# Rows of A and R copied by DMA inside SBUF in place of ScalarE copies

## The chip, the cores and the metric

The kernel runs on one core of one Trainium2 chip. The metric is the device time of one execution, in microseconds (us). A core has five engines that run side by side, each with its own in-order instruction stream: TensorE (PE in the profile, its weight loads PEld), VectorE (DVE), ScalarE (ACT), GpSimd (POOL) and SyncE (SP), which here only issues DMA transfers. Sixteen DMA engines move data between HBM and the on-chip memory SBUF, and within SBUF. TensorE writes into PSUM.

## What is computed

A trunk of two residual layers on 256 positions of width 2048. The first layer is a bidirectional RWKV-7 mixer of width 4096 (64 heads of 64), the second a chunked gMLP, and a final RMSNorm closes. The change lies in the first layer, whose core is a recurrence on a 64x64 state per head and direction:

```python
def step(S, inp):
    r_t, w_t, k_t, v_t, a_t, b_t = inp
    sa = jnp.einsum('bhvk,bhk->bhv', S, a_t)
    S = (S * w_t[:, :, None, :]
         + sa[..., None] * b_t[:, :, None, :]
         + v_t[..., None] * k_t[:, :, None, :])
    y = jnp.einsum('bhvk,bhk->bhv', S, r_t)
    return S, y
```

Here r, k and v come from one input projection (with a mix of neighbouring positions), w and a-related rates from two low-rank projections, a is -kk, b is kk times a rate, and the two directions use their own w and rates. The outputs are normalised per head, a bonus term is added, the result is gated and projected back to 2048.

## The kernel before

The recurrence runs in chunks of 64 positions. Within a chunk it becomes matrix products: for a batch of four heads (two 128-row tiles, `l`), two directions (`d`) and four chunks (`c`) there are 16 units for each of the two heads that share a tile (`h`). There are 16 such batches, and each passes through three steps one period apart, so that in a period batch p gets its weights projected and its factors made (`mains`, `rates`, `factors`, `early_grams`), batch p-1 is made ready for the recurrence (`before`, `values`, `transposed_factors`) and batch p-2 runs it (`after`, which is `chain` and `finish`).

The names that matter:

- `AR` holds the scaled A rows (q = 0) and R rows (q = 1) of a batch. Head h lies in partitions 64h to 64h+63 (`H[h]`), and the last two axes are q and 64 positions, so one unit's A or R row is 64 floats, 256 bytes, on a partition. It has two buffers.
- `grams` multiplies `BK` with `AR` on TensorE (`gp`, line 584) and VectorE masks the product into `Gs` (line 589), which has 2C = 128 columns for each unit and two buffers.
- `inverses` (line 611 on) copies quarter blocks of `Gs` out with ScalarE (`Dt`, line 623, and `NQ`, line 624) and builds from them the inverse `TTs` of a unit-triangular matrix; VectorE does its substitution in 31 pairs of instructions (`TD` and `X`, lines 639 and 641). Once the blocks are out, the upper 64 partitions' first 64 columns of `Gs` are free and get the A rows (line 633).
- `values` (line 666 on) transposes V into the lower half of `SUV` and puts the R rows into `RC` (line 684), of which there is one.
- `chain` goes through the four chunks. In each it forms `xp` from `Gs` (A rows above, masked products below) and `SUV` (line 713), copies it to `Xs` with ScalarE (718), forms `uu` with `TTs` (722), copies that into `SUV` (724), forms the state `sp` (729) and the outputs `yp` (716 with `RC`, from the second chunk on, and 731), and carries the state on through `SJ` (736 to 741).

Weights come as f32 tiles `raw_w...` of 512 KB by SyncE's queue (line 145), are cut into a high and a low part by a ScalarE cast (`whi`, 150) and a VectorE subtraction (`wlo`, 151), and TensorE multiplies three products for each pair (lines 165 to 167). There are two raw buffers in this stage and three of each part, so a load is let go by the subtraction of the load two before it. Each batch has four projections (k, r, v, g) of four loads each, and one smaller load `wu`.

The code is written as generators that yield planned times, and a scheduler with a timeline model then sets the order of each engine's instructions. The order is fixed when the program is built; at run time an engine goes through its own list and waits at semaphores.

Of the kernel before, what the change touches and what calls it, by code (L numbers as in the profile page):

```python
# [22 lines left out]
def trunk(tc, x, norm_g, final_norm_g, w_in, mu_prev, mu_next, w0, w_up, a0, a_up, k_k, k_a, r_k,  # L23
          ln_w, ln_b, w_out, g_w_in, g_ln_g, g_ln_b, g_w_s, g_b_s, g_w_out, out):
    nc = tc.nc
    V, S, G, PE = nc.vector, nc.scalar, nc.gpsimd, nc.tensor
# [9 lines left out]
    C = 64  # L36
# [23 lines left out]
    def sm(name, tag="pg", bufs=2):  # L60
        return psm.tile([P, 512], F32, tag=tag, name=name, bufs=bufs)
# [250 lines left out]
    H = [slice(0, 64), slice(64, 128)]  # L312
# [31 lines left out]
    RC = c2.tile([P, 2, 16, C], F32, name="RC")  # L344
# [266 lines left out]
    def inverses(b, f):  # L611

        Gs, AR = f["Gs"], f["AR"]

        def lane(name):
            return se.tile([P, 16 * 33], F32, tag="ln", name=f"{name}{b}", bufs=3)

        Dt = lane("Dt")[:, :512].rearrange("p (t u) -> p t u", u=16)
        NQ = sc.tile([P, 16, 32], F32, tag="vy", name=f"NQ{b}", bufs=2)
        for h in range(2):  # L620
            for q in range(2):
                r0 = h * 64 + q * 32
                S.copy(Dt[r0:r0 + 32].rearrange("p t u -> p u t"), Gs[q * 32:q * 32 + 32, h, :, q * 32:q * 32 + 32])
            S.copy(NQ[h * 64:h * 64 + 32], Gs[0:32, h, :, 32:64])
        yield TSUB[0]
        La = se.tile([P, 32, 32], F32, tag="La", name=f"La{b}")
        V.transpose(La, Dt.unsqueeze(2).to_broadcast([P, 32, 2, 16]))
        xs = lane("X")
        G.memset(xs[:, :512], 0.0)
        G.tensor_scalar(xs.rearrange("p (m r) -> p m r", r=33)[:, :, 0:32:16], diag, 1.0, None, ALU.mult)  # L630
        X = xs[:, :512].rearrange("p (s t) -> p s t", t=16)
        for h in range(2):
            S.copy(Gs[H[0], h, :, 0:C], AR[H[h], :, :, :, 0].rearrange("p d l c t -> p (d l c) t"))
        TD = lane("TD")[:, :512]
        for j in range(31, 0, -1):
            yield TSUB[1] - (TSUB[1] - TSUB[0] - 2) * j / 31
            m, n = j // 2, 16 - j // 2
            tv = TD[:, :j * n].rearrange("p (s t) -> p s t", t=n)
            V.tensor_tensor(tv, La[:, j, 0:j].unsqueeze(2).to_broadcast([P, j, n]),  # L639
                            X[:, j:j + 1, m:].to_broadcast([P, j, n]), ALU.mult)  # L640
            V.tensor_tensor(X[:, 0:j, m:], X[:, 0:j, m:], tv, ALU.add)  # L641
        yield TSUB[1]
        Tn = lane("Tn")[:, :512]
        V.transpose(TD.rearrange("p (u t h) -> p t h u", t=16, h=2), X.rearrange("p s t -> p t s"))
        V.transpose(Tn, TD)
        TD, Tn = [t.rearrange("p (u t) -> p u t", t=32) for t in (TD, Tn)]
        qp = sm(f"qp{b}", "pq", 1).rearrange("p (u t) -> p u t", t=32)
        R0 = [slice(h * 64, h * 64 + 32) for h in range(2)]
        R1 = [slice(h * 64 + 32, h * 64 + 64) for h in range(2)]
        yield TQ[0]  # L650
        for u in range(16):
            for h in range(2):
                PE.matmul(qp[R1[h], u], NQ[R0[h], u], Tn[R0[h], u], start=True, stop=True)
        for h in range(2):
            S.copy(NQ[R1[h]], qp[R1[h]])
        yield TQ[1]
        for u in range(16):
            for h in range(2):
                PE.matmul(qp[R0[h], u], NQ[R1[h], u], TD[R1[h], u], start=True, stop=True)
        yield TQ[1] + 2  # L660
        for h in range(2):
            S.copy(TTs[R0[h], h, :, 32:64], qp[R0[h]])
            S.copy(TTs[R0[h], h, :, 0:32], TD[R0[h]])
            S.copy(TTs[R1[h], h, :, 32:64], TD[R1[h]])

    def values(b, f):

        yield 72
        Vt = f["Vt"]
        SUV = sc.tile([P, 2, 2, NC, 2, C], F32, tag="SUV", name=f"SUV{b}")  # L670
        G.memset(SUV[H[0], :, :, 0].rearrange("p d l h v -> p (d l) (h v)"), 0.0)
        vp = sm(f"vp{b}", "pq", 1).rearrange("p (m n) -> p m n", n=P)
        for cl in range(2):
            for tt in range(TT):
                PE.transpose(vp[:, cl * TT + tt], Vt[:, cl, tt * P:(tt + 1) * P], ident)
        for d in range(2):

            rows_ = SUV[H[1], d].rearrange("p l c h n -> p (l c) (h n)")
            if d == 1:
                rows_ = rows_[:, ::-1]  # L680
            for half in range(2):
                S.copy(rows_[:, half::2], vp[H[half]])
        for h in range(2):
            S.copy(RC[H[0], h], f["AR"][H[h], :, :, :, 1].rearrange("p d l c t -> p (d l c) t"))
        f.update(SUV=SUV)

    def chain(b, f):
# [99 lines left out]
    def before(b, f):  # L787
        yield from grams(b, f, 1)
        yield from inverses(b, f)
# [119 lines left out]
    for p in range(NB + 2):  # L909
        act = [mains(plan[p], st) if p <= NB else early_out()]  # L910
        if p == 0:
            act.append(low_rank())
        if p < NB:
            act += [rates(p, st[p]), factors(p, st[p]), early_grams(p, st[p])]
        if 0 < p <= NB:
            act += [before(p - 1, st[p - 1]), values(p - 1, st[p - 1]), transposed_factors(p - 1, st[p - 1])]
        if p > 1:
            act.append(after(p - 2, st[p - 2]))
        act = [[0.0, i, g] for i, g in enumerate(act)]
        while act:  # L920
            cur = min(act, key=lambda a: a[:2])
            try:
                cur[0] = max(cur[0], next(cur[2]))
            except StopIteration:
                act.remove(cur)
# [204 lines left out]
    for tt in range(TT):  # L1130
        rstd2 = rms(total(part2[:, tt:tt + 1], f"ssq2_{tt}", hp), f"rstd2_{tt}", hp, V)
        for m in range(NM):
            h = h1[m][:, tt]
# [37 lines left out]
```

## Time and profile before

| | us |
|---|---|
| median of three timed runs | 2244.96 |
| lowest and highest of them | 2243.38, 2249.34 |
| the profiled execution's own time | 2240.81 |
| its span, first to last instruction | 2238.7 |
| granted TensorE clock, mean | 0.993 |
| line 633, ScalarE copy Gs<-AR, each | 1.04 |
| line 684, ScalarE copy RC<-AR, each | 1.05 |
| line 150, cast of one weight tile, each | 1.05 |
| weight load of 512 KB, issue to landing | 3.7 to 3.8 |

The recurrence stage, with all copies of lines 633 and 684, runs from about 88 to 1305 us of the span. Behind it come the rest of the output projection and the second layer. A row of the timeline or of the chain of waits has the start in us, the length in us, the engine, the line and the operation or tile; a bracket at its end tells how long the engine was idle before it and what ended that. A group's row has the busy time in us and the mean length in ns, and behind the second bar the idle time before it. A row of the waits has the engine and line that waited, what ended the wait, the us in total, the times and the longest.

### The profile page before, as it was taken

To read this page: it belongs to the slowest core of one execution; us is meant where nothing else is said; L and a number is where in the kernel's file an instruction comes from. 1 tells how busy PE (TensorE), PEld (TensorE's weight loads), DVE (VectorE), ACT (ScalarE), POOL (GpSimd) and SP (SyncE) were. 2 spreads that over 40 slices of the span, in tenths; PEclk is the share of its full clock that TensorE was granted. 3 is DMA by queue.
4 is the path that set the end of the run, shared out by engine and by line. 5 is a ranking of instruction groups with operands and counts; after the bars stand their busy time and mean duration, and the time that the engine had idled before them with its cause. 6 is when DMAs were issued, how large, how long until landed. Compare 5 with 4: busy or idle time off the path is not lost.

```text
span 2238.7 us, 48543 instructions
## 1 busy us (share of the span) xinstructions
PE 2185.6 (98%) x19984; PEld 1949.8 (87%) x19984; DVE 1613.5 (72%) x3121; ACT 1403.4 (63%) x2192; POOL 188.9 (8%) x230
## 2 busy tenths in 40 slices
PE   7999999999999999999999999999999999999998
PEld 7898899989999999999999977778888888888886
DVE  5787688878877977887797774475546777777444
ACT  6657777777768777776877774464444444444443
POOL 2210100101011101101110100000000000000000
PEclk9999999999999999999999999999999999999999
DMA  5444234333334344434344455586776666666664
GB/s 165 137 129 130 82 113 119 98 108 116 115 115 119 112 125 117 121 109 127 110 121 117 140 175 183 177 262 190 215 213 191 195 193 197 189 193 197 194 196 156
DMA packets 286126, 339.22 MB, mean 152 GB/s; under 512 B 11600, under 2 KB 233552, under 8 KB 285776
## 3 DMA queue, kind: packets, MB, share of 16 engines
q1 hardware_dynamic: 265648, 314.88, 46.5%
q10 hardware_dynamic: 20256, 21.24, 3.3%
q8 instruction: 157, 2.57, 0.5%
q14 instruction: 65, 0.53, 0.1%
HBM read 329.78 MB, written 6.29 MB: 150 GB/s over the span
## 4 chain that ended last, share of the span: by engine, by line
PE 70%; ACT 10%; DMA 9%; DVE 8%; issue 3%; POOL 0%; ACTq 0%; SPq 0%; POOLq 0%; DVEq 0%
PE uacc L204 5%; PE gacc L204 5%; DMA raw_o<-in_rwkv_w_out_dram 4%; PE oacc L166 3%; PE oacc L167 3%; PE oacc L165 3%; PE gp L584 3%; PE uacc L206 3%; PE gacc L206 3%; PE vacc L166 3%; PE vacc L167 3%; PE vacc L165 3%; PE accv L166 3%; PE accv L167 3%; PE accv L165 2%
## 5 line engine op out<-in xcount | busy, mean ns | idle before, releaser
L204 PE MATMUL uacc<-z,whi_u 128*128 128x512 f32 x512 | 179.0, 394 | 0.0
L204 PE MATMUL gacc<-z,whi_g 128*128 128x512 f32 x512 | 177.3, 393 | 0.0
L165 PE MATMUL accv<-zh,whi_wv 128*128 128x256 f32 x512 | 151.8, 296 | 7.0 <-ACT whi_wv L150 7.0
L165 PE MATMUL acck<-zh,whi_wk 128*128 128x256 f32 x512 | 150.9, 295 | 1.4 <-ACT whi_wk L150 1.4
L167 PE MATMUL acck<-zh,wlo_wk 128*128 128x256 f32 x512 | 148.5, 290 | 3.1 <-DVE wlo_wk L151 3.1
L167 PE MATMUL accv<-zh,wlo_wv 128*128 128x256 f32 x512 | 150.5, 294 | 0.8 <-DVE wlo_wv L151 0.5
L166 PE MATMUL accv<-zl,whi_wv 128*128 128x256 f32 x512 | 150.9, 295 | 0.0
L165 PE MATMUL accg<-zh,whi_wg 128*128 128x256 f32 x512 | 150.2, 293 | 0.0
L167 PE MATMUL accg<-zh,wlo_wg 128*128 128x256 f32 x512 | 148.8, 291 | 0.5 <-DVE wlo_wg L151 0.5
L167 PE MATMUL accr<-zh,wlo_wr 128*128 128x256 f32 x512 | 148.4, 290 | 0.2 <-DVE wlo_wr L151 0.2
L166 PE MATMUL acck<-zl,whi_wk 128*128 128x256 f32 x512 | 147.4, 288 | 0.0
L165 PE MATMUL accr<-zh,whi_wr 128*128 128x256 f32 x512 | 146.8, 287 | 0.3 <-ACT whi_wr L150 0.3
L166 PE MATMUL accg<-zl,whi_wg 128*128 128x256 f32 x512 | 146.1, 285 | 0.0
L166 PE MATMUL accr<-zl,whi_wr 128*128 128x256 f32 x512 | 146.0, 285 | 0.0
L206 PE MATMUL uacc<-z,wlo_u 128*128 128x256 f32 x512 | 142.4, 284 | 0.0
L206 PE MATMUL gacc<-z,wlo_g 128*128 128x256 f32 x512 | 140.2, 279 | 0.0
L151 DVE TENSOR_TENSOR wlo_v<-raw_v,whi_v 128x1024 fp32r<-128x1024 f32 x64 | 78.4, 1225 | 80.4 <-ACT whi_v L150 80.4
L151 DVE TENSOR_TENSOR wlo_o<-raw_o,whi_o 128x1024 fp32r<-128x1024 f32 x64 | 78.2, 1224 | 77.7 <-ACT whi_o L150 77.5
L639 DVE TENSOR_TENSOR TD<-La,X 128x126 f32<-128x126 f32 (+22 forms) x496 | 125.6, 253 | 11.2
L641 DVE TENSOR_TENSOR X<-X,TD 128x126 f32<-128x126 f32 (+22 forms) x496 | 124.9, 252 | 10.0
L151 DVE TENSOR_TENSOR wlo_p<-raw_p,whi_p 128x1024 fp32r<-128x1024 f32 x60 | 73.9, 1231 | 75.7 <-ACT whi_p L150 75.7
L150 ACT CAST whi_p<-raw_p 128x1024 fp32r<-128x1024 f32 x60 | 63.1, 1051 | 91.5 <-PE oacc L167 87.3
(333 smaller groups left out, 6936.9 us busy)
## 6 DMA issues: line engine op xcount, KB each, us to landing
raw_wk<-in_rwkv_w_in_dram SPq DMA_DIRECT2D x64, 512.0 KB, 3.8
raw_wr<-in_rwkv_w_in_dram SPq DMA_DIRECT2D x64, 512.0 KB, 3.7
raw_wv<-in_rwkv_w_in_dram SPq DMA_DIRECT2D x64, 512.0 KB, 3.7
raw_wg<-in_rwkv_w_in_dram SPq DMA_DIRECT2D x64, 512.0 KB, 3.7
raw_o<-in_rwkv_w_out_dram SPq DMA_DIRECT2D x64, 512.0 KB, 3.8
raw_v<-in_gmlp_w_in_dram SPq DMA_DIRECT2D x64, 512.0 KB, 3.7
raw_u<-in_gmlp_w_in_dram SPq DMA_DIRECT2D x64, 512.0 KB, 3.5
raw_g<-in_gmlp_w_in_dram SPq DMA_DIRECT2D x64, 512.0 KB, 3.6
```

What stands on the lines that cost most here:

```text
L150: latest[0] = S.copy(hi, raw)
L151: latest[1] = V.tensor_tensor(lo, raw, hi.bitcast(F32), ALU.subtract)
L165: PE.matmul(acc, a[0], b[0], start=first, stop=False, skip_group_check=True)
L166: PE.matmul(acc, a[0], b[1], start=False, stop=False, skip_group_check=True)
L167: PE.matmul(acc, a[1], b[0], start=False, stop=last, skip_group_check=True)
L204: PE.matmul(acc.rearrange("p h t -> p (h t)"), hi[:, j, cs], zc[:, k].rearrange("p h t -> p (h t)"), start=k == 0, stop=False, skip_group_ ...
L206: PE.matmul(acc[:, 0], lo[:, j, cs], zc[:, k, 0], start=False, stop=k == KT - 1, skip_group_check=True)
L584: PE.matmul(gp[h][:, c].rearrange("p q t -> p (q t)"), BK[H[h], d, cl, c].rearrange("p q t -> p (q t)"), AR[H[h], d, cl, c].rearrange("p q ...
L639: V.tensor_tensor(tv, La[:, j, 0:j].unsqueeze(2).to_broadcast([P, j, n]), X[:, j:j + 1, m:].to_broadcast([P, j, n]), ALU.mult)
L641: V.tensor_tensor(X[:, 0:j, m:], X[:, 0:j, m:], tv, ALU.add)
```

## The change

The four ScalarE copies of a batch, two of A rows (line 633) and two of R rows (line 684), go. Four DMA transfers take their place, issued from SyncE's queue at the end of `values`, one for each head h and for A and R. Each moves 64 partitions of 16 rows of 256 bytes, 256 KB, from `AR` to `Gs` or `RC`, all inside SBUF.

```diff
         X = xs[:, :512].rearrange("p (s t) -> p s t", t=16)
-        for h in range(2):
-            S.copy(Gs[H[0], h, :, 0:C], AR[H[h], :, :, :, 0].rearrange("p d l c t -> p (d l c) t"))
         TD = lane("TD")[:, :512]
...
                 S.copy(rows_[:, half::2], vp[H[half]])
+
         for h in range(2):
-            S.copy(RC[H[0], h], f["AR"][H[h], :, :, :, 1].rearrange("p d l c t -> p (d l c) t"))
+            for dst, q in ((f["Gs"][H[0], h, :, 0:C], 0), (RC[H[0], h], 1)):
+                nc.sync.dma_start(dst, f["AR"][H[h], :, :, :, q].rearrange("p d l c t -> p (d l c) t"))
         f.update(SUV=SUV)
```

The scheduler orders the transfers like other work, so on SyncE's queue the two for `Gs` and the two for `RC` stand in different places. The rows below are a program's instructions in order: line, operation, out<-in, shape. The number right behind a name is the batch (in `Gs10`, `raw_wr11`), that after an underscore is a counter. Line numbers behind 633 are two lower in the changed kernel, and the new transfers have line 684 there.

On ScalarE, before, in the period in which batch 10 is made ready and batch 9 runs its chain:

```order
L724 COPY SUV9_11712<-uu9_0_11822 64x4x64 x2
L623 COPY Dt10_11845<-Gs10_11534 32x16x32 x2
L624 COPY NQ10_11846<-Gs10_11534 32x512
L623 COPY Dt10_11845<-Gs10_11534 32x16x32 x2
L624 COPY NQ10_11846<-Gs10_11534 32x512
L150 CAST whi_wr11_0_11875<-raw_wr11_0_11873 128x1024
L633 COPY Gs10_11534<-AR10_11178 64x16x64
L741 COPY SUV9_11712<-SJ9_0_11902 64x4x64 x2
L633 COPY Gs10_11534<-AR10_11178 64x16x64
L150 CAST whi_wr11_4_11934<-raw_wr11_4_11932 128x1024
L395 ACTIVATE kt11_11989<-acck11_11746,c0_174 128x256
L150 CAST whi_wr11_8_12012<-raw_wr11_8_12010 128x1024
```

The same place on ScalarE in the changed kernel:

```order
L718 COPY Xs9_0_11784<-xp9_0_11775 128x256
L150 CAST whi_wr11_0_11873<-raw_wr11_0_11871 128x1024
L623 COPY Dt10_11845<-Gs10_11532 32x16x32 x2
L624 COPY NQ10_11846<-Gs10_11532 32x512
L623 COPY Dt10_11845<-Gs10_11532 32x16x32 x2
L624 COPY NQ10_11846<-Gs10_11532 32x512
L724 COPY SUV9_11710<-uu9_0_11822 64x4x64 x2
L150 CAST whi_wr11_4_11932<-raw_wr11_4_11930 128x1024
L150 CAST whi_wr11_8_12010<-raw_wr11_8_12008 128x1024
L395 ACTIVATE kt11_11987<-acck11_11746,c0_174 128x256
```

The two copies of line 633 are gone, the first cast of r weights has moved ahead of the Dt and NQ copies, and the SUV copies of the first chunk have moved behind them. In this period 47 projection matmuls (41 of k, 6 of r) stand on TensorE between the `uu` products of that chunk and the `yp` and `sp` products that use the SUV copies.

On SyncE's queue, before, from the middle of a k projection's loads on:

```order
L145 DMA raw_wk12_8_12851<-in_rwkv_w_in_dram 128x4x256
L145 DMA raw_wk12_12_12908<-in_rwkv_w_in_dram 128x4x256
L145 DMA raw_wr12_0_12977<-in_rwkv_w_in_dram 128x4x256
L145 DMA raw_wr12_4_13036<-in_rwkv_w_in_dram 128x4x256
L145 DMA raw_wr12_8_13114<-in_rwkv_w_in_dram 128x4x256
L145 DMA raw_wr12_12_13175<-in_rwkv_w_in_dram 128x4x256
```

The changed kernel's queue, from the g projection of the period before to the same place:

```order
L684 DMA RC_333<-AR10_11176 64x16x64 x2
L145 DMA raw_wg10_8_12581<-in_rwkv_w_in_dram 128x4x256
L145 DMA raw_wg10_12_12665<-in_rwkv_w_in_dram 128x4x256
L145 DMA raw_wk12_0_12763<-in_rwkv_w_in_dram 128x4x256
L145 DMA raw_wk12_4_12802<-in_rwkv_w_in_dram 128x4x256
L145 DMA raw_wk12_8_12851<-in_rwkv_w_in_dram 128x4x256
L145 DMA raw_wk12_12_12908<-in_rwkv_w_in_dram 128x4x256
L145 DMA raw_wr12_0_12975<-in_rwkv_w_in_dram 128x4x256
L145 DMA raw_wr12_4_13034<-in_rwkv_w_in_dram 128x4x256
L684 DMA Gs11_12636<-AR11_12280 64x16x64 x2
L145 DMA raw_wr12_8_13112<-in_rwkv_w_in_dram 128x4x256
L145 DMA raw_wr12_12_13173<-in_rwkv_w_in_dram 128x4x256
```

Two RC transfers now stand in the middle of the g loads, and two Gs transfers ahead of the third r load. In batch 10 the two Gs transfers stand one load later, behind the third r load. The transfers for Gs wait for the NQ copies, those for RC for the last product that reads RC in the chain of the batch before.

## Prediction

> **What bounds the kernel now.** I read the page first, then the busy time by stretches, then the list of TensorE's waits in the recurrence stage, then the chain of waits and the timelines around the copies that the change removes.
>
> ```profile
> PE 2185.6 (98%) x19984; PEld 1949.8 (87%) x19984; DVE 1613.5 (72%) x3121; ACT 1403.4 (63%) x2192; POOL 188.9 (8%) x230
> ...
> 240.00:316.00 76.00, 71.85 (x792) 65.93 (x793) 61.73 (x149) 57.97 (x101) 6.92 (x10) 0.96 0.35 101
> 1000.00:1076.00 76.00, 75.59 (x941) 70.55 (x939) 63.16 (x148) 57.19 (x99) 10.45 (x10) 1.00 0.41 121
> 1500.00:1600.00 100.00, 100.00 (x449) 82.63 (x448) 54.04 (x55) 48.52 (x57) 0.70 (x1) 1.00 0.66 190
> ```
>
> The rows of the stretches give, after the length, the busy time of PE, PEld, DVE, ACT and POOL, then the granted clock, the DMA share and GB/s. The first two stretches lie in the recurrence stage: ScalarE (ACT) is busy 57 to 58 of 76 us there, TensorE 71.9 early on and 75.6 later. So TensorE is the bound, and ScalarE has some 18 us to spare in each stretch. Time taken off ScalarE is worth only what TensorE waits for it. TensorE's waits between 88 and 1310 us, the stage that holds every removed copy:
>
> ```profile
> PE accv L165 <- ACT whi_wv L150: 7.0, 4, 3.3
> PE uu L722 <- ACT Xs L718: 4.8, 10, 0.9
> ...
> PE accr L165 <- ACT whi_wr L150: 0.3, 1, 0.3
> ```
>
> These are the first two and the last of 17 rows (us in all, times, longest). All 17 add up to 27.1 us, 1.2% of the run, and those with ACT as the releaser to 18.4 us. That is the most that a lighter ScalarE can give back, unless other waits fall with it.
>
> **What is removed.**
>
> ```profile
> L684 ACT COPY RC<-AR 64x1024 f32<-64x1024 f32 x32 | 33.6, 1051 | 0.3
> L633 ACT COPY Gs<-AR 64x1024 f32<-64x1024 f32 x32 | 33.4, 1044 | 0.3
> ```
>
> There are 64 copies of about 1.05 us, so 67.0 us of ScalarE's 1403.4 go, 4.2 us in each of 16 batches. The views of these two lines name nobody who waited for them. What matters is who stood behind them. In the steady part of the stage the chain of waits runs like this (start, duration, engine, tile, line):
>
> ```profile
> 877.83 1.09 ACT Dt L623
> 878.98 1.03 issue
> 880.01 0.62 ACT NQ L624
> 880.65 1.08 ACT Dt L623
> 881.74 1.08 ACT Dt L623
> 882.84 0.63 ACT NQ L624
> 883.48 1.06 ACT whi_wr L150
> 884.57 1.23 DVE wlo_wr L151
> 885.82 3.63 DMA raw_wr<-in_rwkv_w_in_dram
> 889.47 1.05 ACT whi_wr L150
> 890.84 0.69 PE uu L722 x16
> ```
>
> ScalarE in the same place:
>
> ```profile
> 884.44 1.04 ACT L633 COPY Gs<-AR 64x1024 f32<-64x1024 f32 x1
> 885.39 0.82 ACT L741 COPY SUV<-SJ 64x256 f32<-64x256 f32 x2
> 886.12 1.04 ACT L633 COPY Gs<-AR 64x1024 f32<-64x1024 f32 x1
> ...
> 889.47 1.05 ACT L150 CAST whi_wr<-raw_wr 128x1024 fp32r<-128x1024 f32 x1 [0.74 <-DMA raw_wr<-in_rwkv_w_in_dram]
> ```
>
> The copies of L633 run at 884.44 and 886.12, and yet the chain does not pass through them: it goes from NQ through a cast, VectorE's subtraction, and the load which that subtraction lets go. ScalarE stood idle 0.74 us before the cast at 889.47 because the load had not landed. Without the copies it would stand idle there about 2.8 us, and Xs and uu would come no sooner. In the steady batches I therefore put the gain at **0**.
>
> In the early batches a copy does stand right ahead of something that TensorE waits for:
>
> ```profile
> 270.79 1.04 ACT L633 COPY Gs<-AR 64x1024 f32<-64x1024 f32 x1
> 271.74 1.04 ACT L150 CAST whi_wv<-raw_wv 128x1024 fp32r<-128x1024 f32 x1
> ```
>
> ```profile
> 269.65 0.28 PE L166 MATMUL accv<-zl,whi_wv 128*128 128x256 f32 x1
> 269.77 0.28 PE L167 MATMUL accv<-zh,wlo_wv 128*128 128x256 f32 x1
> ...
> 272.83 0.39 PE L165 MATMUL accv<-zh,whi_wv 128*128 128x256 f32 x1 [1.20 <-ACT whi_wv L150]
> ```
>
> Here TensorE waits 1.20 us for a cast that the copy held up by about 1.04. The list above counts four waits of this kind (whi_wv). I take 4 x 1.04 = **4.2 us** as the gain, with 0 and 18.4 us as the ends; I stay near the low end since only this place shows the copy itself in the way.
>
> **What is added: 64 transfers of 256 KB, four a batch, on SyncE's queue.** The trace of before has no transfer with rows of 256 bytes, so I bound one. The stretch at 1000 moves mostly 1 KB rows: 16 x 0.41 / (121 GB/s / 1024) = 56 ns of one DMA engine for a row. At 1500 the rows are 2 KB: 16 x 0.66 / (190 / 2048) = 114 ns. Cost goes by bytes there, so a 256-byte row should take about 14 ns, and at most the 56 of a 1 KB row. A transfer has 1024 such rows, 64 for each of 16 engines: 0.9 us, at most 3.6. I take 0.9, since the two stretches go by bytes. Four add 3.6 us to a DMA share of 0.41 of a 76 us stretch, 14 at most: the share becomes 0.46, at most 0.59, so there is room.
>
> [...]
>
> How long may they take? The nearest transfer of this size, and the readers on TensorE:
>
> ```profile
> oT<-OT ACTq DMA_DIRECT2D x16, 256.0 KB, 2.5
> ```
>
> ```profile
> 711.49 0.37 ACTq L785 DMA_DIRECT2D oT<-OT  x1
> ```
>
> ```profile
> 915.30 0.57 PE L716 MATMUL yp<-SUV,RC 128*64 128x64 f32 x13
> ...
> 948.64 0.45 PE L713 MATMUL xp<-SUV,Gs 128*64 128x64 f32 x8
> ...
> 964.13 0.28 PE L716 MATMUL yp<-SUV,RC 128*64 128x64 f32 x2
> ```
>
> The same bytes out of SBUF land 2.5 us after issue. Batch 10's A rows, ready to be overwritten at 883.5 (end of NQ), are first read at 948.6, 65 us later. Its R rows may be written once batch 9's last read is over, near 915.9, and are read at 964.1, 48 us later. Neither reader can notice 2.5 us, or 10. This cover hides the whole latency.
>
> **What the wait does to the queue.** SyncE's queue is in order, so weight loads stand behind a Gs transfer that waits for NQ. But the next load needs a raw buffer that an earlier cast and subtraction release. In the changed order that cast stands behind the NQ copies on ScalarE in 30 of 32 cases (the ScalarE rows of batch 10, in the section on the change, show one: NQ, then the cast of the second r tile, whose buffer the fourth load takes), so the load could not have gone sooner: cost 0. For RC the wait is on TensorE's last read; the same comparison with the Xs copy of that step finds the wait over before the releasing cast, or one to five short ScalarE rows after it, which VectorE's 1.23 us subtraction mostly covers. Issuing the nearest transfer, oT's, took its queue 0.37 us, so four cost SyncE about 1.5 us a batch, in a queue that mainly waits for VectorE: 0. If that cover were gone, a load would be late by the wait itself, a few us, once in the batch.
>
> **Sum.** The profiled execution took 2240.81 us (span 2238.7). 2240.81 - 4.2 = 2236.6. The median of the three timed runs is 2244.96, 4.15 above the profiled one, so against that median: **2241 us**, a change of 0.2%. About 0.3% (6.7 us) is what a measurement of this kernel can tell from no change.
>
> **Rivals.**
>
> *The early batches recover more (faster).* Stretch 240:316 has TensorE busy 71.85 us of 76, against 75.59 in 1000:1076. Moving ScalarE's work earlier may take away most of the 18.4 us and not just the four places: with two thirds, 12 us, it gives 2233. Against it: in the list the waits for Xs, ten of them, are at most 0.9 us each, and the steady ones are set by a load.
>
> *The reshuffled order makes TensorE wait (slower).* Taking out the copies made the scheduler re-order much of ScalarE's stage. In batch 10 the two SUV copies now stand behind the whole Dt/NQ block, where before they were ahead. The block takes 4 x 1.08 + 2 x 0.62 = 5.6 us. TensorE has 47 projection matmuls between the uu products and their use; the rows at 269.65 and 269.77 start 0.12 us apart, so that cover is 5.6 us. SUV itself takes about 0.8, and the chain shows 1.03 us lost inside the block waiting for the mask. So TensorE waits up to 0.8 + 1.0 = 1.8 us in such a batch; it decides whether the block begins more than that before uu ends. Should half of the 16 batches have such a place, 14 us are lost, beside the 4.2 gained: 2255. For it: the same form is in batches 10, 12 and 14. Against it: the block may begin early, since it waits only for the mask.
>
> *Short rows are dear (slower).* If a 256-byte row costs as much as a 1 KB row or more, a Gs transfer holds the engines 3.6 us or more. The second one of a pair goes out when NQ ends, at 883.47, and the load at 885.82, so the load would be late by some 2 us, and the chain above passes through that load. In half of the batches the pair stands ahead of this load (batch 11), in half behind it (batch 10): 8 x 2 = 16 us, 2257. [...] No row of the trace speaks for it.
>
> That the change would not do what it says I leave out: the order shows the copies gone and the transfers there.
>
> **How the numbers follow.** Forecast, nearly no change: 0.45, 2241. More recovered: 0.31, 2233, at best 2227. Order: 0.19, 2255. Dear rows: 0.05, 2257. The forecast lies within 0.3% of 2244.96 (2238.2 to 2251.7), so faster has 0.31, same 0.45, slower 0.24. The range 2228 to 2259 takes in most of the faster case and the slower ones up to their prices.
>
> **What would show it.** ACT's busy time should fall by 67 us to about 1336. The DMA share in a steady stretch should go to about 0.46. The list of TensorE's waits should keep its sum within a few us of 27.1, and uu should still wait for Xs behind a cast that waits for its load. The landing time of the new transfers should be about 2 to 3 us; 5 or more would mean dear rows. Waits of yp or sp for SUV in the later batches would show the reshuffled order at work. The forecast is wrong if the steady stretches, like the one at 1000, gain or lose more than half a us a batch.

## Result and profile after

The changed kernel takes 2229.55 us, the median of six runs (2229.11 to 2231.46). Measured in rounds against the kernel before on the same chip the ratio is 0.9942, 95% interval 0.993 to 0.9953: **0.6% faster**. The kernel before took 2241.96 to 2242.65 us (medians) beside the experiments below, so the 2244.96 ahead of the prediction was on the high side. The time lies inside the range, and near the rival "the early batches recover more" (2233), not at the forecast of 2241. Two slow executions enter no ratio, one of the kernel before (2353.31 us) and one of e8_pause (3501.02 us at a mean clock of 0.555). The profiled execution took 2229.16 us with a span of 2227.4, against 2240.81 and 2238.7: 11.3 us of span.

The first part of the page, and the same three stretches as before:

```profile
PE 2179.0 (98%) x19984; PEld 1944.7 (87%) x19984; DVE 1608.1 (72%) x3121; ACT 1345.2 (60%) x2128; POOL 171.8 (8%) x230
```

```profile
240.00:316.00 76.00, 75.42 (x831) 70.31 (x829) 68.52 (x165) 53.16 (x94) 11.88 (x13) 1.00 0.47 122
1000.00:1076.00 76.00, 74.35 (x868) 69.79 (x861) 64.47 (x153) 51.39 (x90) 6.93 (x11) 1.00 0.50 133
1500.00:1600.00 100.00, 100.00 (x447) 82.74 (x446) 51.75 (x49) 46.07 (x50) 0.00 (x0) 1.00 0.67 192
```

ScalarE lost 58 us of work and its 64 copies. TensorE was busy 71.85 of 76 us in the early stretch and is now busy 75.42, and the granted clock there went from 0.96 to 1.00. In the stretch at 1000 TensorE is 1.24 us less busy than before, and the second layer (1500) is untouched. So the gain shows in the early stretch. The list of TensorE's waits between 88 and 1310 us, first three and last of 16 rows:

```profile
PE yp L731 <- ACT SUV L724: 2.8, 4, 1.1
PE accg L167 <- DVE wlo_wg L151: 2.4, 1, 2.4
PE uu L722 <- ACT Xs L718: 2.4, 6, 0.6
...
PE up L165 <- ACT TH L481: 0.2, 1, 0.2
```

The 16 rows add up to 21.1 us, against 27.1. The waits for whi_wv, 7.0 us before, are 1.1 now. The same list by stretches shows where the 6.0 us went. Between 240 and 700 us, before (first two and last of nine rows):

```profile
PE accv L165 <- ACT whi_wv L150: 3.4, 2, 2.2
PE gp L584 <- DVE Gs L589: 1.8, 2, 1.4
...
PE accr L165 <- ACT whi_wr L150: 0.3, 1, 0.3
```

and after, all five:

```profile
PE vp L673 <- ACT TTs L660: 1.3, 2, 0.9
PE yp L731 <- ACT SUV L724: 0.7, 2, 0.4
PE hs_k L406 <- ACT SQ L492: 0.6, 1, 0.6
PE uu L722 <- ACT Xs L718: 0.2, 1, 0.2
PE up L165 <- DVE NK L503: 0.2, 1, 0.2
```

That is 11.6 us before and 3.0 after. Between 88 and 240 the sums are 9.1 and 9.4, between 700 and 1310 they are 6.3 and 8.6. So 8.6 us of waits went in one stretch and 2.6 came in the others: a net of 6.0, while the span is 11.3 shorter. The rest of this text is about that difference, and about the rows that follow.

**The clock.** Before, two stretches of the trace with what came ahead of them (length, busy time of PE, PEld, DVE, ACT, POOL, granted clock, DMA share, GB/s):

```profile
176.00:183.00 7.00, 3.92 (x88) 3.67 (x86) 2.19 (x4) 6.89 (x8) 0.85 (x2) 0.97 0.20 68
183.00:190.00 7.00, 6.31 (x30) 6.01 (x31) 6.06 (x16) 6.56 (x11) 0.00 (x0) 0.54 0.52 149
...
275.00:278.00 3.00, 3.00 (x16) 3.00 (x15) 2.44 (x7) 1.08 (x3) 0.00 (x0) 0.50 0.66 189
```

The first matmuls of the second stretch, and some of the third, on TensorE:

```profile
183.17 0.58 PE L165 MATMUL accv<-zh,whi_wv 128*128 128x256 f32 x1 [3.26 <-ACT whi_wv L150]
...
275.27 0.41 PE L165 MATMUL accv<-zh,whi_wv 128*128 128x256 f32 x1
275.49 0.41 PE L166 MATMUL accv<-zl,whi_wv 128*128 128x256 f32 x1
```

The prediction's rows at 269.65 and 269.77 show the same kind of matmul starting 0.12 us apart. Here they start 0.22 us apart, while the granted clock is 0.50: after a stretch in which TensorE had been much idle (3.92 us busy of the 7 from 176, 4.80 of the 7 from 267.7) it ran at half speed for 6.8 us from 182.6 and for 3.4 us from 274.7, though at 275 nothing was late any more (3.00 us busy of 3). The wait of 1.20 us at 272.83, which the prediction priced at 1.04, was followed by the half-speed stretch at 275. After the change the early stretch 240:316 has the full clock. Over the whole execution the list of cores says

```profile
core 0: 2238.7 us, clock 0.993
```

before, and after

```profile
core 0: 2227.4 us, clock 0.995
```

The lost clock is (1 - 0.993) x 2238.7 = 15.7 us before and (1 - 0.995) x 2227.4 = 11.1 after: 4.5 us less, give or take 2 for the rounding of the two clocks. With the 6.0 us of waits that makes 10.5 of the 11.3 us. The page of the profile splits it differently: TensorE is busy 6.6 us less and idle 4.7 us less, which is the 11.3. So the waits that the list names fell by more than the idle time did, and the sum above closes partly by luck. The lost clock also counts the end of the execution, where no product is left: from 2231 us on before the clock is 0.69 with TensorE busy 0.00, some 2.4 us lost that cost nothing. After the change it is the same 2.4, so the difference stands.

**The transfers.** The new line 684 after, by kind of instruction (ns shortest, median, longest; start of the first and the last), with its landing times:

```profile
L684 SPq DMA_DIRECT2D RC<-AR x32: 596/663/1619, 85.5 to 1294.4; - x32
L684 SPq DMA_DIRECT2D Gs<-AR x32: 590/596/665, 108.5 to 1256.3; - x32
L684 SPq EVENT_SEMAPHORE  x26: 17/17/4396, 85.5 to 1294.4; - x26
...
DMA to landing us min/median/max: 3.4/4.1/7.5
```

SyncE's queue in the table of DMA queues (packets, MB, share of 16 engines), before:

```profile
q1 hardware_dynamic: 265648, 314.88, 46.5%
```

and after:

```profile
q1 hardware_dynamic: 332208, 331.66, 51.6%
```

In engine time that is 0.516 x 16 x 2227.4 - 0.465 x 16 x 2238.7 = 1733 us more, for 65536 rows of 256 bytes: 26 ns a row, all that they slowed in others included. The prediction took 14, at most 56.

### The profile page after: what moved, and what is told of

It is laid out like the page before. It is cut to its first block, busy times and chain, and to the rows that moved or that the text cites. A ratio compares the mean times of both kernels' runs of the same rounds, so it can differ in the third digit from the quotient of the medians.

```text
span 2227.4 us, 48630 instructions
## 1 busy us (share of the span) xinstructions
PE 2179.0 (98%) x19984; PEld 1944.7 (87%) x19984; DVE 1608.1 (72%) x3121; ACT 1345.2 (60%) x2128; POOL 171.8 (8%) x230
## 4 chain that ended last, share of the span: by engine, by line
PE 69%; ACT 10%; DMA 9%; DVE 8%; issue 3%; ACTq 0%; SPq 0%; POOL 0%; POOLq 0%; DVEq 0%
PE uacc L204 5%; PE gacc L204 5%; DMA raw_o<-in_rwkv_w_out_dram 3%; PE oacc L166 3%; PE oacc L167 3%; PE oacc L165 3%; PE gp L584 3%; PE gacc L206 3%; PE uacc L206 3%; PE vacc L167 3%; PE vacc L165 3%; PE vacc L166 3%; ACT Dt L623 2%; PE accv L165 2%; PE accg L167 2%
```

## The experiments

Three theories at first. **1**: a lighter ScalarE in the early batches gives the whole gain, and the transfers cost about nothing. **2**: the gain is luck of the new order. **3**: the transfers cost something that hides a larger gain. Each ratio is to the kernel before. The edits shown are against the changed kernel for e1, e2, e3, e4, e8, e9, e11 and e12, and against the kernel before for e5, e6, e7 and e10. A span is that of one execution; those of one kernel differ by several us (e9_aonly_again's four run from 2217.4 to 2226.3).

| run | what moves A and R rows | us, median | ratio, 95% interval | profiled span |
|---|---|---|---|---|
| the change | DMA, all batches | 2229.55 | 0.9942 (0.993 to 0.9953) | 2227.4 |
| e1_none | nothing | 2229.1 | 0.9946 (0.9931 to 0.9961) | 2225.1 |
| e2_early | DMA in batches 0 to 6, ScalarE in the rest | 2230.35 | 0.9953 (0.9936 to 0.9969) | 2226.8 |
| e3_late | ScalarE in batches 0 to 6, DMA in the rest | 2241.64 | 0.9995 (0.9985 to 1.0004) | 2242.4 |
| e4_aonly | A by DMA, R by ScalarE | 2222.75 | 0.9912 (0.9895 to 0.9928) | 2221.5 |
| e5_pool | GpSimd copies | 2240.77 | 0.9992 (0.9975 to 1.0009) | 2242.2 |
| e6_both | ScalarE, and the transfers to a spare tile | 2243.52 | 1.0004 (0.9989 to 1.0018) | 2243.6 |
| e7_order | ScalarE, one planned time changed | 2241.33 | 0.9994 (0.9978 to 1.0011) | 2239.2 |
| e9_aonly_again | as e4_aonly | 2224.1 | 0.9917 (0.9898 to 0.9937) | 2220.3 |
| e10_ronly | R by DMA, A by ScalarE | 2238.92 | 0.9983 (0.9974 to 0.9993) | 2240.7 |
| e11_aearly | A by DMA in batches 0 to 6, the rest by ScalarE | 2234.27 | 0.9967 (0.9954 to 0.998) | 2232.5 |
| e12_rpoolq | DMA, R's from GpSimd's queue | 2235.9 | 0.997 (0.9956 to 0.9984) | 2232.4 |

**What do the transfers cost?** e1_none leaves A and R rows out of Gs and RC altogether:

```diff
-    G.memset(RC[64:128], 0.0)
+    G.memset(RC, 0.0)
...
-        for h in range(2):
-            for dst, q in ((f["Gs"][H[0], h, :, 0:C], 0), (RC[H[0], h], 1)):
-                nc.sync.dma_start(dst, f["AR"][H[h], :, :, :, q].rearrange("p d l c t -> p (d l c) t"))
```

> The 64 copies are left out and nothing takes their place, so Gs keeps its masked products where the A rows belong and RC holds zeros: the output is not the reference's. This is the worth of taking the copies off ScalarE, without the transfers. Theory 1 (ScalarE's time in the early batches is what the change gave back, the transfers cost next to nothing): 0.99 to 0.995 of before, within 4 us of the changed kernel's 2229.6. Theory 2 (the gain came by chance from a new order): anywhere from 2225 to 2255. Theory 3 (the transfers cost something, hidden in the net gain): 8 us or more below 2229.6.

2229.1 us, the same as the change. e6_both asks from the other side: ScalarE copies as before, and four transfers of the same size that nobody needs.

```diff
+    scr = c2.tile([P, 16, C], F32, name="scr")
...
             S.copy(RC[H[0], h], f["AR"][H[h], :, :, :, 1].rearrange("p d l c t -> p (d l c) t"))
+            nc.sync.dma_start(scr[H[0]], f["AR"][H[h], :, :, :, 0].rearrange("p d l c t -> p (d l c) t"))
+            nc.sync.dma_start(scr[H[1]], f["AR"][H[h], :, :, :, 1].rearrange("p d l c t -> p (d l c) t"))
```

> ScalarE keeps its 64 copies, and four transfers a batch of the same shape as the change's go into a scratch tile that nobody reads. This adds the transfers' price alone. Theory 1: within 4 us of before. Theory 3: 8 us or more slower. Theory 2: between 15 us faster and 10 us slower by the new order.

1.0004 of before, interval 0.9989 to 1.0018. The stretch at 1000 of e1_none, without any transfer,

```profile
1000.00:1076.00 76.00, 75.89 (x1051) 70.97 (x1051) 60.09 (x139) 58.86 (x103) 5.82 (x10) 1.00 0.40 114
```

has a DMA share of 0.40 against the change's 0.50. So the transfers are real load, and their net price in time is nil within the intervals, about 3 us. Theory 3, which asked for 8 us or more, falls. e6_both's zero is itself a balance: against before its waits between 88 and 1310 fell from 27.1 to 22.3 us, and TensorE's busy time rose from 2185.6 to 2191.5.

**Which batches gain?** e2_early and e3_late put the condition `b < 7` or `b >= 7` ahead of the transfers, and the ScalarE copies in the other batches:

```diff
+        if not (b < 7):
+            for h in range(2):
+                S.copy(Gs[H[0], h, :, 0:C], AR[H[h], :, :, :, 0].rearrange("p d l c t -> p (d l c) t"))
...
-            for dst, q in ((f["Gs"][H[0], h, :, 0:C], 0), (RC[H[0], h], 1)):
-                nc.sync.dma_start(dst, f["AR"][H[h], :, :, :, q].rearrange("p d l c t -> p (d l c) t"))
+            if b < 7:
+                for dst, q in ((f["Gs"][H[0], h, :, 0:C], 0), (RC[H[0], h], 1)):
+                    nc.sync.dma_start(dst, f["AR"][H[h], :, :, :, q].rearrange("p d l c t -> p (d l c) t"))
+            else:
+                S.copy(RC[H[0], h], f["AR"][H[h], :, :, :, 1].rearrange("p d l c t -> p (d l c) t"))
```

> Transfers for batches 0 to 6 alone, ScalarE copies for batches 7 to 15. Theory 1, with the gain in the early batches: 10 to 15 us faster than before, as the changed kernel. If the gain comes evenly from all batches: 5 to 7 us faster. Theory 2: no telling, between 15 us faster and 10 us slower.

> Transfers for batches 7 to 15 alone, ScalarE copies for batches 0 to 6. Theory 1: within 4 us of before, since the steady batches are bound by TensorE. Evenly: 6 to 8 us faster. Theory 2: between 15 us faster and 10 us slower, with no relation to the run with the early batches.

The early seven give the whole gain (0.9953), the late nine none (0.9995). The waits between 240 and 700 us add up to 3.5 us in e2_early and to 12.6 in e3_late, beside 3.0 in the change and 11.6 before. This is what theory 1 asks for, as far as the change goes as a whole. But fewer waits in this stretch do not by themselves make a kernel faster: e6_both, with all copies still on ScalarE, has 5.8 us of them, and e5_pool, the next run, 4.9, and neither gains.

**Is it ScalarE's relief, or its order?** e5_pool relieves ScalarE by putting the same copies on GpSimd:

```diff
-            S.copy(Gs[H[0], h, :, 0:C], AR[H[h], :, :, :, 0].rearrange("p d l c t -> p (d l c) t"))
+            G.tensor_copy(Gs[H[0], h, :, 0:C], AR[H[h], :, :, :, 0].rearrange("p d l c t -> p (d l c) t"))
...
-            S.copy(RC[H[0], h], f["AR"][H[h], :, :, :, 1].rearrange("p d l c t -> p (d l c) t"))
+            G.tensor_copy(RC[H[0], h], f["AR"][H[h], :, :, :, 1].rearrange("p d l c t -> p (d l c) t"))
```

> The 64 copies moved to GpSimd in place of ScalarE, no transfers. ScalarE has the same relief as in the changed kernel. Theory 1: 10 to 15 us faster than before, unless a GpSimd copy takes so long that the chain waits for it (then the list of TensorE's waits would name POOL). Theory 2: anywhere from 15 us faster to 10 us slower.

No gain: 0.9992. ScalarE's busy time is that of the change (1345.3 us), so relief alone isn't enough, and theory 1 missed here. A GpSimd copy stands in that engine's order: ahead of its RC copies GpSimd sat idle 252.0 us for the last product that reads RC (yp, line 716), and the work behind them with it. That this ate the gain isn't shown, and the sign that the expectation named for it is absent: no row of TensorE's waits names POOL. TensorE's waits fell to 23.8 us in all, and its busy time rose to 2189.2. e7_order keeps the ScalarE copies of before and disturbs only the order, by one planned time in `values`:

```diff
-        yield 72
+        yield 71
```

> The kernel before with the planned time of the step that transposes V and copies the R rows moved from 72 to 71, so that only the order of instructions differs. Theory 1: within 4 us of before. Theory 2: several us off, to either side, as far as the change itself.

0.9994. One disturbed order gives no gain. It is one sample, and it does not clear order of having a part, as the next runs show.

**A and R apart.** e4_aonly leaves R to ScalarE:

```diff
-            for dst, q in ((f["Gs"][H[0], h, :, 0:C], 0), (RC[H[0], h], 1)):
-                nc.sync.dma_start(dst, f["AR"][H[h], :, :, :, q].rearrange("p d l c t -> p (d l c) t"))
+            nc.sync.dma_start(f["Gs"][H[0], h, :, 0:C], f["AR"][H[h], :, :, :, 0].rearrange("p d l c t -> p (d l c) t"))
+            S.copy(RC[H[0], h], f["AR"][H[h], :, :, :, 1].rearrange("p d l c t -> p (d l c) t"))
```

> A rows by transfer, R rows by ScalarE copies as before. Theory 1: half of ScalarE's relief, 5 to 8 us faster than before. Theory 2: anywhere from 15 us faster to 10 us slower.

Theory 1 missed here too: half the relief gives more than the whole, 0.9912. Two theories were set against each other on this. **Q**: an R transfer waits on SyncE's queue for the chain's last reader of RC and holds the weight loads behind it. **O**: each arrangement gets an order of its own, and its small TensorE pauses with it. The same program was run once more, with the other half beside it (A by ScalarE, R by DMA, the edit mirrored), with A by DMA in the early batches only, and with the R transfers taken off SyncE's queue:

```diff
-            for dst, q in ((f["Gs"][H[0], h, :, 0:C], 0), (RC[H[0], h], 1)):
-                nc.sync.dma_start(dst, f["AR"][H[h], :, :, :, q].rearrange("p d l c t -> p (d l c) t"))
+            nc.sync.dma_start(f["Gs"][H[0], h, :, 0:C], f["AR"][H[h], :, :, :, 0].rearrange("p d l c t -> p (d l c) t"))
+            for d in range(2):
+                nc.gpsimd.dma_start(RC[H[0], h, d * 8:(d + 1) * 8],
+                                    f["AR"][H[h], d, :, :, 1].rearrange("p l c t -> p (l c) t"))
```

> The kernel with A moved by transfers and R by ScalarE copies once more, to see whether its 2222.75 us is a property of the program. Both theories: 2222 to 2225 us, since the order of every engine is fixed in the program; 2229 or more would mean that the first run was chance. Span some 5 to 6 us below that of the change.

> R moved by transfers, A by ScalarE copies: the other half. Theory Q (an R transfer waits on SyncE's queue for the chain's last reader of RC, up to 4.4 us, and holds the weight loads behind it): the R half costs what A alone gained over the change, so R alone is 5 to 9 us worse than A alone plus the lost relief: 2238 to 2245 us. Theory O (each arrangement has an order of its own, and its sum of small TensorE pauses is luck): anywhere between 2223 and 2242, and TensorE's waits and half-clock windows give its place.

> A moved by transfers in batches 0 to 6 alone, everything else by ScalarE copies. If the gain of A alone lies in the early batches, like that of the whole change: 2222 to 2227 us. If the late batches of A alone gain too: 2229 to 2236. Theory O: a place of its own between 2223 and 2242 that neither rule gives.

> The change with the R transfers issued from GpSimd's queue (in halves of 512 rows) instead of SyncE's, so that no weight load stands behind them. Theory Q: 2221 to 2225 us, as with A alone or better. Theory O: 2227 to 2232 like the change, or a place of its own; issuing on GpSimd may cost that engine some us a batch, which it has free at 8% busy.

The gain of A alone came back (0.9917). R alone gains 0.0017, as theory Q put it. But e1_none, which has no R transfer that anything could stand behind, is no better than the change. So **theory Q falls**: R's transfers do not cost by holding weight loads. e12_rpoolq, which Q needs to be as good as A alone, is even worse than the change. It weighs less, since it brings a wait of its own: GpSimd idles 245.4 us ahead of the R transfers for the last product that reads RC.

What remains is the order of the instructions, and one place in ScalarE's order shows how it differs. In the program of before, the SUV copies of a batch's first chunk stand behind the next batch's Dt and NQ block in the first 7 of 15 cases and ahead of it in the other 8. With A alone by DMA they are behind it in 6 and inside it in 4, in the change behind it in 13 (in e1_none, e3_late and e5_pool too), in e10_ronly and e12_rpoolq in all 15. This is the form of the rival "the reshuffled order". TensorE's waits between 700 and 1310 us, A alone (all three rows):

```profile
PE oacc L165 <- ACT whi_o L150: 1.4, 1, 1.4
PE oacc L166 <- DVE wlo_o L151: 0.6, 1, 0.6
PE oacc L165 <- ACT BT L607: 0.4, 1, 0.4
```

the change (first two):

```profile
PE yp L731 <- ACT SUV L724: 2.1, 2, 1.1
PE uu L722 <- ACT Xs L718: 2.1, 5, 0.6
```

e12_rpoolq (first two):

```profile
PE yp L733 <- ACT SUV L726: 6.3, 4, 2.3
PE uu L724 <- ACT Xs L720: 3.0, 5, 1.0
```

With A alone TensorE waits for no copy from uu to SUV in these batches (0.2 us in e4_aonly), and for 0.3 us in before; with the copies behind the block it waits 2.1 us in the change and 6.3 in e12_rpoolq. And the waits for Xs, which are in the list of before as

```profile
PE uu L722 <- ACT Xs L718: 3.4, 8, 0.7
```

are gone with A alone. Yet this place does not decide the time. e2_early and e11_aearly have the copies behind the block in 6 cases as A alone has, and e6_both in 5, and their ratios are 0.9953, 0.9967 and 1.0004. With A alone TensorE is then busy all of the steady stretch, as in neither of the two kernels. From 700 to 1100 us, before, then the change, then A alone (e9_aonly_again):

```profile
700.00:1100.00 400.00, 397.35 (x4946) 370.48 (x4946) 332.73 (x770) 303.91 (x519) 55.19 (x54) 1.00 0.41 118
```

```profile
700.00:1100.00 400.00, 396.94 (x4880) 370.61 (x4879) 324.28 (x758) 283.72 (x488) 36.66 (x50) 1.00 0.49 132
```

```profile
700.00:1100.00 400.00, 399.98 (x4970) 373.33 (x4969) 330.42 (x764) 299.72 (x509) 48.37 (x50) 1.00 0.46 127
```

So the late batches do gain from A's transfers, if R stays: with A by DMA in the early batches only (e11_aearly) the ratio is 0.9967, with A in all batches 0.9917, and the intervals do not overlap. That is also what e11_aearly's expectation said for this case (2229 to 2236; 2234.27 came). The starts of the k projections say the same. That of batch 8, at 632.1 us before, comes 7.8 us sooner with A alone (e9_aonly_again) and 11.7 sooner in the change; that of batch 15, at 1180.4, comes 21.0 and 17.3 sooner. The orders differ, so such a point is good to a few us. Theory O stands as the one not refuted, but it allows nearly any time and did not forecast any of these. Why leaving R on ScalarE is better than moving it is not shown.

**What isn't settled.** The waits do not carry all of it. The 15 rows of e9_aonly_again between 88 and 1310 add up to 19.7 us and its mean clock is 0.995, as in the change; that explains 1.4 of the 7.1 us by which its span is shorter. From 700 us on it waits 6.2 us less than the change, but between 88 and 700 it waits 4.9 more (17.3 against 12.4). The rest is in this line:

```profile
PE 2172.8 (98%) x19984; PEld 1937.7 (87%) x19984; DVE 1612.3 (73%) x3121; ACT 1374.3 (62%) x2160; POOL 187.4 (8%) x230
```

TensorE is busy 6.2 us less than in the change, with the same 19984 matmuls at the same mean clock. e6_both shows the opposite:

```profile
PE 2191.5 (98%) x19984; PEld 1949.9 (87%) x19984; DVE 1612.3 (72%) x3121; ACT 1398.9 (62%) x2192; POOL 191.9 (9%) x230
```

It is busy 5.9 us more than before, at a clock of 0.994 and with waits of 22.3 us. So TensorE's busy time differs by some 6 us either way, below what the list of waits shows. Most of this lies in two groups, the `gp` products of `grams` and the transposes `yt` of the outputs. The rows of `gp`, the change and then e9_aonly_again:

```profile
L584 PE MATMUL gp<-AR,BK 64*128 64x128 f32 x1024 | 97.2, 289 | 3.0 <-DVE Gs L589 1.7 <-DVE BK L555 1.3
L584 PE MATMUL gp<-AR,BK 64*128 64x128 f32 x1024 | 91.6, 290 | 1.9 <-DVE Gs L589 1.9
```

That is 5.6 us less at the same mean length, so the products overlap more; e4_aonly has 92.6. `yt` goes from 20.4 to 19.5. In e6_both the two take 100.8 and 27.4 us, against 98.8 and 24.2 before. But `gp` takes only 91.1 in e10_ronly, which is hardly faster than before, so no one group follows the times of all runs. What makes these products stand closer together stays open.

**Does a pause cost more than itself?** e8_pause adds to the second layer of the changed kernel, where the clock is full, eight transposes whose input ScalarE has only just written:

```diff
-    def gated(name, dst, tmp):
+    def gated(name, dst, tmp, pause=None):
...
+        if pause is not None:
+            PE.transpose(acc[0].rearrange("p h t -> p (h t)")[:, :P], pause, ident)
...
-        gated(f"gacc{g}", Ga, Gt)
+        gated(f"gacc{g}", Ga, Gt, {1: Gt[:, 1, 0:P], 3: U[:, 1, 0:P]}.get(g % 4))
```

> The changed kernel with eight transposes put ahead of the gate products of the second layer. Each makes TensorE wait for what ScalarE and VectorE made of the product before: four for a plain copy (some 1 to 2 us), four for the whole chain up to the gelu (some 4 to 6 us). The outputs stay as they are. If a pause costs only its own length, the kernel is slower by the sum of the pauses, some 25 us, and the granted clock stays at 1. If a pause is followed by a stretch at half clock, the time lost is more than the pauses by 1.7 us for each such stretch of 3.4 us, up to 14 us in all, and the clock of the stretches shows it.

The profiled execution took 2266.04 us, 36.9 more than the change's. The waits added, and the stretches ahead of and behind a long pause, then a short one:

```profile
PE gacc L1064 <- ACT U L1080: 16.4, 4, 4.1
PE gacc L1064 <- ACT Gt L1067: 5.6, 4, 1.4
```

```profile
1756.00:1763.00 7.00, 2.91 (x18) 2.34 (x17) 4.63 (x7) 3.57 (x6) 0.00 (x0) 1.00 0.65 194
1764.00:1767.00 3.00, 3.00 (x12) 2.58 (x11) 0.00 (x0) 0.00 (x0) 0.00 (x0) 0.55 0.02 5
1706.00:1713.00 7.00, 5.61 (x34) 4.74 (x34) 5.50 (x8) 3.18 (x5) 0.00 (x0) 1.00 0.71 228
1713.00:1720.00 7.00, 7.00 (x42) 6.18 (x41) 3.26 (x4) 2.73 (x3) 0.00 (x0) 1.00 0.45 139
```

Behind a pause of 4.1 us the clock is halved, behind one of 1.4 us in a busy stretch it is not; so it is behind all four of each. The mean clock fell to 0.989. By the same working as above the lost clock is (1 - 0.989) x 2264.3 = 24.9 us, 13.8 more than in the change. With 22.0 us of waits that is 35.8 of the 36.9. Not all of the 13.8 comes from the pauses: the half-speed stretches behind the four long ones last 3.4 or 6.8 us each, which is about 10 us lost. Two more, 3.4 us each at 67 and 1483 us (clocks 0.51 and 0.50), have no pause of the edit ahead of them, and the change's clock at these times is 1.00. Still, a term that the prediction lacked is shown here by itself, in one execution; this run has no ratio.

## Why the prediction came out low

- **TensorE is the bound, and ScalarE's time is worth what TensorE waits for it**: right in the first part: 58 us came off ScalarE and 11 off the span. The second part leaves out the clock and the time of the products themselves; in e5_pool the same 58 us came off ScalarE and nothing off the time.
- **4 x 1.04 = 4.2 us in the early batches**: the place was right, the size was not, and this is the term that failed; the measured gain is about 13 us (0.9942 of 2242). The waits for whi_wv fell from 7.0 to 1.1 us, and other waits of the same batches fell too: 8.6 us between 240 and 700. The prediction stayed near the low end because it found one place where the copy itself stood in the way. How each of those waits hung on a copy further ahead was not traced, and after e5_pool and e6_both it stays open whether ScalarE's relief or the new order took them away. The rival had put the gain at two thirds of 18.4 us, 12 us. It met the time partly by luck: the waits for ACT fell from 18.4 to 13.0 us, by 5.4, and clock and other terms made up the rest.
- **"The most that a lighter ScalarE can give back" is 18.4 us**: this counted waits alone. The lost clock behind them, 15.7 us before, was a second thing that could fall with them, and 4.5 us of it did. The prediction had the row for it (a clock of 0.96 in 240:316 against 1.00 at 1000) and used only its busy time.
- **Steady batches gain 0**: as a net result right, since the late batches alone measured 0.9995. The sign that the prediction named, more than half a us a batch in a stretch like the one at 1000, came out both ways: TensorE is 1.24 us less busy in that stretch, but only 0.41 from 700 to 1100 us, some five batches (397.35 and 396.94). The reason given did not hold. The place that the prediction walked through stands 12.2 us sooner in the changed kernel (Dt at 865.62 against 877.83), and behind the Dt and NQ copies ScalarE has:

```profile
871.96 2.00 ACT L150 CAST whi_wr<-raw_wr 128x1024 fp32r<-128x1024 f32 x2
```

  The second of these two casts is the one ahead of which ScalarE was to idle about 2.8 us. It ran right behind the first, without a wait for its load; the new order had put the r cast ahead of them in front of the block. ScalarE idles 1.17 us for the next r load, at 879.29. So the load did not set this place once the order had changed. With A alone by DMA no wait for Xs is left from 700 us on, where before there were 3.4 us of them, and the late batches do gain. A steady gain was there to be had, and the change doesn't have it.
- **The reshuffled order**: taken for a rival with 14 us, it is in the change too, at 2.1 us of waits for SUV in the late batches (2.8 in all) and not at 1.8 in each. It turned no gain into a loss. One row was misread for it: the 1.03 us at 878.98, taken for a wait for the mask inside the block, is marked issue in the chain, and ScalarE is at work on its second Dt copy then. The wait for the mask lies ahead of the block:

```profile
877.83 2.17 ACT L623 COPY Dt<-Gs 32x512 f32<-32x512 f32 x2 [1.06 <-DVE Gs L589]
```

- **256-byte rows**: 26 ns where 14 was taken and 56 was the upper end. The DMA share went to 0.50, not 0.46, and the transfers land in 4.1 us (median; 3.7 for Gs, 5.2 for RC), not 2 to 3. The 4.1 is still under the 5 that would have meant dear rows, RC's own median isn't. As computed, the readers come tens of microseconds later, and nothing of it reaches the end. By their engine time and by the run's time the rows were not dear: 26 ns is less than twice the estimate by bytes, and e1_none shows no cost in time. The rival's 2 us for a late load were also high for its own rows: 883.47 + 3.6 is 1.3 us past 885.82.
- **Waits on SyncE's queue cost 0**: right within about 3 us, by e1_none. Issue was underrated: 0.60 and 0.66 us for a transfer, against oT's 0.37, and one semaphore wait of up to 4.4 us.
- **ACT's busy time, to about 1336**: 1345.2. The 64 copies went, but a copy overlaps the instruction behind it (884.44 + 1.04 us ends 0.09 us after 885.39, in the prediction's rows), so their summed lengths are more than the busy time that they filled: 64 x 0.09 = 5.8 of the 8.8 us.

## What to carry to other kernels

Where TensorE is the bound, read the granted clock of a stretch beside its busy time: in the kernel before, the wait of 1.20 us at 272.83, close behind one of 0.90 at 270.95, was followed by 3.4 us at a clock of 0.50, so it could be paid for twice, once as a wait and once as half speed behind it; in e8_pause a wait of 4.1 us was followed by a clock of 0.55, one of 1.4 us by the full clock. Work taken off a second engine is best judged by undoing it in parts: here half of the change was worth more than all of it, and a run with the same relief by another engine was worth nothing. So the wait list of one kernel did not tell what the change would be worth, and why the R half takes back part of the gain is not settled. **Moving A alone by DMA and leaving R to ScalarE beats both kernels**, at 2222.75 and 2224.1 us, ratios 0.9912 and 0.9917. Its eight executions took 2215.93 to 2228.06 us, the change's six 2229.11 to 2231.46.

## What the runs showed of the hardware

- In the traces of before and of the change the granted clock fell to 0.50 for 3.4 or 6.8 us after a stretch in which TensorE was much idle: ahead of each of the ten falls in the two traces that come before the last product it was busy 4.32 to 5.83 us of 7. Two stretches of before that lie right ahead of such a fall:

```profile
251.00:258.00 7.00, 5.09 (x40) 4.42 (x40) 6.87 (x22) 5.93 (x10) 3.45 (x4) 0.97 0.26 74
462.00:469.00 7.00, 5.83 (x129) 5.32 (x123) 6.25 (x9) 6.26 (x11) 0.00 (x0) 1.00 0.36 109
```

A third such stretch, and the one right behind it, where the clock did not fall:

```profile
340.00:347.00 7.00, 4.76 (x50) 4.45 (x45) 2.94 (x6) 6.89 (x9) 1.67 (x1) 1.00 0.29 99
347.00:354.00 7.00, 6.86 (x89) 6.38 (x89) 6.22 (x18) 5.43 (x8) 0.00 (x0) 1.00 0.38 102
```

  Between 340 and 347 TensorE was as idle as between 251 and 258, and the clock stayed at 1.00. So idle time came ahead of each fall shown here, but it did not suffice. Nor does the length of a single wait tell: the longest ahead of the fall at 274.7 was 1.20 us, the one that ends at 346.71 was 2.24 us. In the clock record of before, the seven falls ahead of the last product come at 66.5, 114.3, 141.6, 182.6, 257.6, 274.7 and 469.3 us, whole multiples of 3.413 us apart, and six of them last 3.413 us, the one at 182.6 twice that. When idle time is followed by a fall is not shown: from 343.0 to 346.4, one step of the same spacing, TensorE was busy 1.47 us, and no fall followed.
- The same program lost different amounts of clock in two executions: e4_aonly has a mean of 0.993 and a span of 2221.5 us, e9_aonly_again 0.995 and 2220.3. That is some 4 us of clock for 1.2 us of span, so the sum of waits and clock is good to some microseconds only.
- Issuing a transfer of 1024 rows of 256 bytes took SyncE's queue 0.60 us (Gs) and 0.66 (RC) by the median, one of the same bytes in oT took ScalarE's queue 0.37.
